# The last third of a hybrid mixer in one written order, and the final norm in two halves of the tokens

## The chip, the cores and the metric

The kernel runs on one NeuronCore of a Trainium2 chip. The metric is the device time of one execution in microseconds (us), the median of three runs. Its engines each work through a queue of their own: TensorE (PE, matrix products), VectorE (DVE), ScalarE (ACT, activations and copies), GpSimd (POOL) and SyncE (SP, which here only issues DMAs). They meet in semaphores: an instruction waits at the head of its queue until what it reads is written and what it overwrites has been read.

## The reference

One decoder layer for 256 tokens of width 1024, all in float32: two half-step SwiGLU feed-forward networks (FFN, 22 tiles of 128 hidden columns) with a mixer between them, each behind an RMSNorm whose scale, shift and gate come from a product of the condition `c` with `w_ada` ("ada", 9 x 1024 columns), and a final RMSNorm.

```
mod = (c @ w_ada + b_ada)                    # 9 x 1024: shift, scale, gate three times
h = modulate(rmsnorm(x, ffn1_norm), sh1, sc1)
x = x + 0.5 * (1 + g1) * swiglu(h, ffn1_w_gate, ffn1_w_up, ffn1_w_down)
h = modulate(rmsnorm(x, mix_norm), sh2, sc2)
x = x + (1 + g2) * hybrid_mixer(h, ...)
h = modulate(rmsnorm(x, ffn2_norm), sh3, sc3)
x = x + 0.5 * (1 + g3) * swiglu(h, ffn2_w_gate, ffn2_w_up, ffn2_w_down)
return rmsnorm(x, final_norm)
```

The mixer projects `h` to attention queries, keys and values, to the input of an mLSTM (a gated linear recurrence, here over chunks of 64 tokens in matrix form) and to a gate `z`. Half of its output is the RMS-normed attention, the other half `(norm(h_m) + mlstm_skip * x_conv) * silu(z)`; both together go through `w_out` (1024 x 1024).

## The kernel before

Everything stands in transposed form: 128 channels on the partitions, 256 tokens on the free axis; `x_sb` is 8 such tiles. A product in float32 is made of three in a faster format (float32r): a weight piece of 128 x 1024 is split into `whi` (ACT, a rounding copy) and `wlo` (DVE, the rest), the activations into `hh` and `hl`, and `mm3` issues hi x hi, lo x hi, hi x lo. `weights()` hands out the next weight chunk (2048 columns, 1 MB), has the DMA of the chunk three ahead issued and splits up to the end of the next chunk; four raw chunks and five pieces each of `whi` and `wlo` have room, so a split waits until the products of five pieces before are done. PSUM has 8 banks under three tags: "b" 2, "m" 2, "a" 4.

The ada products are jobs in a list. `side(0)` takes one out: a DMA of 512 KB (`ada`, three buffers) and one DVE operation that multiplies it with `c` and sums (`junk`, 128 x 1024). FFN 1 works off some, the mixer the rest.

Where `Ordered.on` of an engine is set, its instructions keep the order in which the program issues them (`keep_in_program_order`); where it is off, a scheduler orders them by its own estimate of their times. Either way, each engine then runs its queue in that order. All compute instructions are issued by `call` of `Ordered`, so the trace gives them all line 55, and tiles tell them apart by name.

The last third of the mixer, in program order: `tiles()` projects the z gate, two tiles of 24 matmuls per chunk, with `shifted` as what follows each (a column `col`, `ht` on DVE, `zs` on ACT); `values(1)` is the last projection of attention values (`va`); `turn(3)` transposes attention probabilities (`pT`), `weigh(2)` and `weigh(3)` multiply them with `va` (`oa`) and square; `m_sums` and `m_vars` are the mLSTM's sums for a head (`cn`, `sq`); `a_out` sums the squares over `ones_h` into a bank, takes Ln and Exp (`rl`, `rr`), refines by one Newton step on DVE (`nw`, `rr`), scales `oa` and splits it into `mix0` and `mix3`; `m_factors` makes four rows of factors (`dd`, `vv`, `rs`, `rows`), `z_silu` takes the SiLU of `zs` (another table of ACT), and `m_spread` and `m_out` spread the rows over the partitions and make the mLSTM's half of the output (`cn`, then `hh`, `hl`). The output projection runs over 4 chunks `c` of `w_out`, 48 matmuls each, into 4 banks; then `residual` adds each tile to x and makes `hh`, `hl` and the square for FFN 2, which follows.

In the kernel before, the written order is on from `weigh(3)` to the z tile behind `a_out`, in `m_factors` and from there to `z_silu`, and around `m_spread` and `m_out`; elsewhere in this part the scheduler decides.

At the end, `residual` multiplies x with the final norm's weight on POOL (`u_out`), `rstd_of` makes the norm's factor for all 256 tokens, and five DVE products each send their tiles out, from SP and ACT in turn (L600 to L604).

Of the kernel before, what the change touches and what calls it, by code (L numbers as in the profile page):

```python
# [14 lines left out]
ALU = mybir.AluOpType  # L15
# [46 lines left out]
def layer(ctx: ExitStack, tc: tile.TileContext, i, out: bass.AP):  # L62
# [237 lines left out]
    def rstd_of(parts, ones=None, tag="m", pre=True, mid=None):  # L300

        ps = bank(tag)[:, 0:T]
        for n, s in enumerate(parts):
            pe.matmul(ps, ones_m if ones is None else ones, s, start=(n == 0), stop=(n == len(parts) - 1))
        r = t256("rr", bufs=2)
        l = t256("rl", bufs=1)
        if pre:
            tables("natural_log_exp_and_others")
        act.activation(l, ps, AF.Ln, bias=eps_t)
        act.activation(r, l, AF.Exp, scale=-0.5)  # L310
        if mid:
            mid()
        newton(r, ps, [P, T], "x")
        return r
# [43 lines left out]
            eng.tensor_tensor(acc, acc, s, ALU.add)  # L358
        return s

    def residual(d, ps, g, k):
        dve.scalar_tensor_tensor(x_sb[:, d], ps, g[:, d:d + 1], x_sb[:, d], ALU.mult, ALU.add)
        if k is None:
            s = add_sq(d, pool)
            pool.tensor_scalar(fin_u[0][:, d], x_sb[:, d], sm[:, C_NF + d:C_NF + d + 1], None, ALU.mult)
            return s
        if k == 1:

            s = add_sq(d, pool)
            for j in range(2 * d - 6, 2 * d - 4) if 3 <= d < 6 else range(d, d + 1) if d >= 6 else ():  # L370
                pre_h(k, j)
        elif d == ND - 1:
            s = add_sq(d, pool)
            pre_h(k, d)
        else:
            pre_h(k, d)
            s = add_sq(d, pool)
        return s
# [26 lines left out]
    def ffn(k, nxt):  # L405
        nfa = 3
        with tc.tile_pool(name=f"g{k}", bufs=1) as gp:
            g2 = gp.tile([P, NF, 2, T], F32R, name=f"g2{k}")
            gh, gl = g2[:, :, 0], g2[:, :, 1]
            if k == 0:  # L410
# [71 lines left out]
                        inner(w, f2, ps[2 * j + f2], 0, False)  # L482
                for d in range(4, 8):
                    w = weights()
                    side(1)
                    outer(w, ps, d, d == 7)

                late = [lambda ft=ft: finish(gh, gl, 8 + ft, ps[ft][:, 0:T], ps[ft][:, T:2 * T])
# [1 line left out]
                for j in range(4):  # L490
                    if j < 2:
                        late.pop(0)()
                        late.pop(0)()
                    w = weights()
                    if j == 3:
                        side(1)
                    for f2 in range(2):
                        ft = 2 * j + f2
                        pb = bank("a")
                        inner(w, f2, pb, 4, True)  # L500
                        o = half[:, ft]
                        dve.tensor_tensor(o, o, pb, ALU.add)
                        finish(gh, gl, ft, o[:, 0:T], o[:, T:2 * T])
# [63 lines left out]
    def side(*on):  # L567

        for o in on:
            if jobs:  # L570
                jobs.pop(0)(o)
# [24 lines left out]
    with tc.tile_pool(name="fin", bufs=1) as fp:  # L596
        u = fin_u[0] = fp.tile([P, ND, T], F32, name="u_out")
        jobs += gate_jobs(2)
        ffn(2, None)
        r = rstd_of([acc, nxt_sq[0]], pre=False)  # L600
        r2 = r.unsqueeze(1).to_broadcast([P, 2, T])
        for n, (a, b) in enumerate(((0, 2), (2, 4), (4, 6), (6, 7), (7, 8))):
            dve.tensor_tensor(u[:, a:b], u[:, a:b], r2[:, 0:b - a], ALU.mult)
            (sp, nc.scalar)[n % 2].dma_start(out[:, a:b], u[:, a:b])  # L604


def mixer(tc, nc, i, mp, L):
# [9 lines left out]
    def mt(shape, name, dt=F32, tag=None, bufs=1):  # L617
        return mp.tile(shape, dt, name=nm(name), tag=tag or name, bufs=bufs)

    def tiles(*done):  # L620

        w = weights()
        for g in range(2):
            pb = bank("b")
            for d in range(8):
                mm3(pb[:, 0:W], w, (g * 8 + d) * P, hh[:, d], hl[:, d], start=(d == 0), stop=(d == 7))
            done[g](pb)
            yield

    def shifted(dst):  # L630

        def done(pb):
            col = tmp.tile([P, 1], F32, tag="col", name=nm("col"), bufs=3)
            act.activation(col, pb[:, T:T + 1], AF.Copy)
            t = t256("ht", bufs=3)
            dve.tensor_tensor(t, r, pb[:, 0:T], ALU.mult)
            act.activation(dst, t, AF.Identity, bias=col)
        return done
# [168 lines left out]
    def m_vars(h):  # L807
        pe.matmul(st["prow"][0:4, T:2 * T], ohc[:, h], st["sq", h], start=False, stop=(h == NH - 1),
                  skip_group_check=True)

    def m_factors():


        prow, em = st["prow"], st["em"]
        act.on = dve.on = True
        dd = mt([NH, T], "dd", tag="R2")
        act.activation(dd, prow[0:4, 0:T], AF.Square, scale=EPS ** 0.5)
        dve.tensor_tensor(dd, dd, em, ALU.max)
        vv = mt([NH, T], "vv", tag="R3")
        dve.scalar_tensor_tensor(vv, prow[0:4, T:2 * T], 1.0 / P, dd, ALU.mult, ALU.add)  # L820
        rs = mt([NH, T], "rs", tag="R1")
        act.activation(rs, vv, AF.Ln)
        act.activation(rs, rs, AF.Exp, scale=-0.5)
        newton(rs, vv, [NH, T], "r", 0.0)
        spread(rs)
# [105 lines left out]
            pool.tensor_tensor(acc2, acc2, s, ALU.add)  # L931

    def a_out():
        r2 = rstd_of([acc2, st["osq"]], ones_h, "a", pre=False)
        for j in range(4):
            o = oa[:, j, 0:T]
            dve.scalar_tensor_tensor(o, o, sm[:, C_AN + j:C_AN + j + 1], r2, ALU.mult, ALU.mult)

        mix3[:] = [mt([P, 3, T], name, F32R, tag="pr", bufs=2) for name in ("mix3h", "mix3l")]
        hilo(*mix0, oa[:, 0, 0:T])  # L940
        hilo(*mix3, oa[:, 1:4, 0:T])
# [49 lines left out]
    turn(2)  # L991
    m_scores(3)
    m_sums(1)
    g = tiles(shifted(zs[:, 0]), shifted(zs[:, 1]))
    side(0, 0, 0, 0, 0, 0)
    next(g)
    next(g0)
    turn(3)
    weigh(2)
    for e in (pe, act, dve):  # L1000
        e.on = True
    weigh(3)
    m_sums(2)
    m_vars(0)
    a_out()
    next(g)
    act.on = dve.on = False
    m_sums(3)
    m_skip()
    m_vars(1)  # L1010
# [6 lines left out]
    next(g)  # L1017
    z_silu(0)
    z_silu(1)
    act.on = dve.on = False  # L1020
    po = [bank(t) for t in ("m", "m", "a", "a")]
    for c in range(4):
        w = weights()
        side(*[0] * (0, 1, 2, 3)[c])
        pe.on = c < 2
        for k2 in range(2):
            k = c * 2 + k2
            for d in range(8):
                mm3(po[d // 2][:, (d % 2) * T:(d % 2 + 1) * T], w, (k2 * 8 + d) * P, *mix(k),
                    start=(c == 0 and k2 == 0 and d % 2 == 0), stop=(c == 3 and k2 == 1))  # L1030
                if (k, d) == (1, 7):
                    m_spread()
                    act.on = dve.on = True
                    m_out(0)
                    m_out(1)
                    act.on = dve.on = False
    side(*[0] * len(jobs))
    act.on = dve.on = True
    L["pre_shift"](2)
    act.on = dve.on = False  # L1040
    for d in range(8):
        nxt_sq[0] = residual(d, po[d // 2][:, (d % 2) * T:(d % 2 + 1) * T], L["gt"][1], 2)


# [84 lines left out]
```

## Time and profile before

| | |
|---|---|
| runs | 534.71, 532.76, 532.58 us; median 532.76 |
| profiled execution | 531.47 us |
| its span in the trace | 529.7 us, 9595 instructions |
| mean granted PE clock | 0.995 of full |
| PE, DVE, ACT, POOL busy | 97%, 80%, 53%, 9% |
| FFN 1 begins / mixer's last third / FFN 2 begins / final norm | 0 / about 262 / 329 / 519.3 us |

Times in the trace's rows are in us from the span's start. The busy time of an engine counts the instructions that run, not the queue's waiting. A row of a timeline gives start, duration, engine, operation and tiles (out<-in); in brackets stands how long the engine stood idle ahead of it and which instruction ended that. Matmuls overlap: two in a row start 0.12 us apart and last 0.28 us each.

### The profile page before, as it was taken

How to read it: one execution, taken by the hardware profiler on the slowest of the kernel's cores; microseconds unless marked ns; L12 is line 12 of the kernel's file. 1: busy time of each engine (PE TensorE's matmuls, PEld its weight loads, DVE VectorE, ACT ScalarE, POOL GpSimd, SP SyncE). 2: the span in 40 equal slices, each digit the busy share in tenths (PEclk: the TensorE clock that was granted, in tenths of full speed). 3: DMA queues.
4: the chain of work that ended last, by engine and by line, in shares of the span. 5: the costliest groups of instructions: out<-in, count | busy, mean ns of one | idle time of the engine just before them, and what ended most of it. 6: DMA issues, size and time to landing. Idle time of an engine off the chain costs nothing.

```text
span 529.7 us, 9595 instructions
## 1 busy us (share of the span) xinstructions
PE 511.9 (97%) x3826; PEld 480.0 (91%) x3826; DVE 422.3 (80%) x703; ACT 282.9 (53%) x484; POOL 45.5 (9%) x60
## 2 busy tenths in 40 slices
PE   8999999999999999999999988999999999999992
PEld 7889999999988889988877888999999999988891
DVE  7799977998889997997869887989887777655423
ACT  4364436655645444569766554865555545544410
POOL 5000000000001110120000001300000000022220
PEclk9999999999999999999999999999999999999997
DMA  8999985677878887783115963578764554464002
GB/s 306 363 368 379 376 357 201 251 278 287 321 294 298 335 329 290 282 354 120 41 41 198 400 227 103 206 301 307 285 241 160 171 215 171 161 220 178 0 1 79
DMA packets 24095, 125.73 MB, mean 237 GB/s; under 512 B 2673, under 2 KB 3185, under 8 KB 14578
## 3 DMA queue, kind: packets, MB, share of 16 engines
q1 hardware_dynamic: 23762, 124.72, 62.4%
q8 instruction: 30, 0.49, 0.4%
q10 hardware_dynamic: 288, 0.39, 0.2%
q14 instruction: 15, 0.12, 0.1%
HBM read 124.05 MB, written 1.05 MB: 236 GB/s over the span
## 4 chain that ended last, share of the span: by engine, by line
PE 87%; DVE 6%; DMA 3%; ACT 2%; issue 1%; SPq 0%; DVEq 0%; ACTq 0%
PE psa L55 44%; PE psb L55 24%; PE psm L55 19%; DVE junk L55 2%; DMA ada<-in_ada 2%; DVE wlo L55 1%; ACT whi L55 1%; DMA x<-in_x 1%; DVE u_out L55 0%; DVE ht L55 0%; ACT sq L55 0%; DVE oa L55 0%; DVE hl L55 0%; DVE nw L55 0%; ACT hh L55 0%
## 5 line engine op out<-in xcount | busy, mean ns | idle before, releaser
L55 ACT ACTIVATE whi<-raw 128x1024 fp32r<-128x1024 f32 (+1 forms) x160 | 166.8, 1047 | 128.1 <-PE psa L55 78.7
L55 DVE TENSOR_TENSOR wlo<-raw,whi 128x1024 fp32r<-128x1024 f32 (+1 forms) x160 | 193.7, 1214 | 45.0 <-ACT whi L55 43.5
L55 PE MATMUL psa<-hh,wlo 128*128 128x256 f32 (+1 forms) x440 | 123.3, 281 | 0.0
L55 PE MATMUL psa<-hh,whi 128*128 128x256 f32 (+1 forms) x440 | 123.1, 282 | 0.0
L55 PE MATMUL psa<-hl,whi 128*128 128x256 f32 (+1 forms) x440 | 122.1, 280 | 0.0
L55 DVE SCALAR_TENSOR_TENSOR junk<-ada,c_bc 128x1024 bf16<-128x1024 f32 x72 | 89.8, 1248 | 11.8 <-DMA ada<-in_ada 11.5
L55 PEld LDWEIGHTS psa<-hh,wlo 128*128 128x128 f32 x440 | 83.1, 189 | 0.1
L55 PEld LDWEIGHTS psa<-hh,whi 128*128 128x128 f32 x440 | 82.9, 189 | 0.0
L55 PE MATMUL psb<-hh,whi 128*128 128x258 f32 (+1 forms) x284 | 82.1, 290 | 0.8 <-ACT whi L55 0.6
L55 PEld LDWEIGHTS psa<-hl,whi 128*128 128x128 f32 x440 | 82.7, 189 | 0.0
L55 PE MATMUL psb<-hh,wlo 128*128 128x258 f32 (+1 forms) x284 | 80.5, 284 | 0.4 <-DVE wlo L55 0.4
L55 PE MATMUL psb<-hl,whi 128*128 128x258 f32 (+1 forms) x284 | 79.6, 282 | 0.0
L55 PE MATMUL psa<-g,whi 128*128 128x512 f32 (+1 forms) x198 | 59.8, 369 | 0.0
L55 PEld LDWEIGHTS psb<-hh,whi 128*128 128x128 f32 x284 | 53.7, 189 | 3.0 <-ACT whi L55 1.0
L55 PEld LDWEIGHTS psb<-hh,wlo 128*128 128x128 f32 x284 | 53.8, 189 | 1.7 <-issue 1.0
L55 PEld LDWEIGHTS psb<-hl,whi 128*128 128x128 f32 x284 | 53.5, 190 | 0.0
L55 PE MATMUL psa<-g,wlo 128*128 128x256 f32 x176 | 45.9, 281 | 0.0
L55 PE MATMUL psm<-hh,whi 128*128 128x256 f32 (+1 forms) x156 | 43.9, 282 | 1.7 <-ACT hh L55 1.7
L55 PE MATMUL psm<-hl,whi 128*128 128x256 f32 (+1 forms) x156 | 43.7, 282 | 0.5 <-DVE hl L55 0.4
L55 PE MATMUL psm<-hh,wlo 128*128 128x256 f32 (+1 forms) x156 | 43.8, 281 | 0.0
L55 PEld LDWEIGHTS psa<-g,whi 128*128 128x128 f32 x198 | 35.2, 188 | 6.2
L55 PEld LDWEIGHTS psa<-g,wlo 128*128 128x128 f32 x176 | 32.1, 188 | 0.6
(251 smaller groups left out, 777.5 us busy)
## 6 DMA issues: line engine op xcount, KB each, us to landing
ada<-in_ada SPq DMA_DIRECT2D x72, 512.0 KB, 5.9
raw<-in_dn SPq DMA_DIRECT2D x22, 1024.0 KB, 4.8
raw<-in_guB SPq DMA_DIRECT2D x19, 1024.0 KB, 4.8
raw<-in_gu SPq DMA_DIRECT2D x18, 1024.0 KB, 7.3
raw<-in_gu SPq DMA_DIRECT2D x8, 512.0 KB, 7.4
raw<-in_wqk SPq DMA_DIRECT2D x4, 1024.0 KB, 6.3
raw<-in_wout SPq DMA_DIRECT2D x4, 1024.0 KB, 7.7
raw<-in_guA SPq DMA_DIRECT2D x4, 768.0 KB, 4.6
```

The source lines that it names most:

```text
L55: r = f(*a, **k)
```

## The change

FFN 1 takes three ada products more (one at d = 7, and two in the loop behind it), so that the mixer has three fewer. In the mixer, the written order is on for PE, ACT and DVE from the first z tiles to the end of the residuals, save for ACT while the weights of c = 1 are handed out; `tiles(apart=True)` can be continued between a tile's matmuls and what follows them; the six ada products in a row become single ones at six places, and those of the output projection one per chunk; `m_out(1)` moves to c = 1; the residual takes x of tile d and then the norm's part of tile d - 1 in turn. The final norm is made for 128 tokens at a time, with four products and four DMAs of 256 KB.

```diff
@@ -358,8 +358,9 @@
             eng.tensor_tensor(acc, acc, s, ALU.add)
         return s
 
-    def residual(d, ps, g, k):
-        dve.scalar_tensor_tensor(x_sb[:, d], ps, g[:, d:d + 1], x_sb[:, d], ALU.mult, ALU.add)
+    def residual(d, ps, g, k, add=True):
+        if add:
+            dve.scalar_tensor_tensor(x_sb[:, d], ps, g[:, d:d + 1], x_sb[:, d], ALU.mult, ALU.add)
         if k is None:
             s = add_sq(d, pool)
             pool.tensor_scalar(fin_u[0][:, d], x_sb[:, d], sm[:, C_NF + d:C_NF + d + 1], None, ALU.mult)
@@ -482,7 +483,7 @@
                         inner(w, f2, ps[2 * j + f2], 0, False)
                 for d in range(4, 8):
                     w = weights()
-                    side(1)
+                    side(*[1] * (1 + d // 7))
                     outer(w, ps, d, d == 7)
 
                 late = [lambda ft=ft: finish(gh, gl, 8 + ft, ps[ft][:, 0:T], ps[ft][:, T:2 * T])
@@ -492,7 +493,7 @@
                         late.pop(0)()
                         late.pop(0)()
                     w = weights()
-                    if j == 3:
+                    if j != 1:
                         side(1)
                     for f2 in range(2):
                         ft = 2 * j + f2
@@ -597,11 +598,27 @@
         u = fin_u[0] = fp.tile([P, ND, T], F32, name="u_out")
         jobs += gate_jobs(2)
         ffn(2, None)
-        r = rstd_of([acc, nxt_sq[0]], pre=False)
-        r2 = r.unsqueeze(1).to_broadcast([P, 2, T])
-        for n, (a, b) in enumerate(((0, 2), (2, 4), (4, 6), (6, 7), (7, 8))):
-            dve.tensor_tensor(u[:, a:b], u[:, a:b], r2[:, 0:b - a], ALU.mult)
-            (sp, nc.scalar)[n % 2].dma_start(out[:, a:b], u[:, a:b])
+
+        pr, sq = [bank("m") for _ in range(2)], nxt_sq[0]
+        lr = [t256(t, bufs=b) for t, b in (("rl", 1), ("rr", 2), ("ht", 3))]
+        H = [slice(0, P), slice(P, T)]
+        for e in (pe, act, dve):
+            e.on = True
+        for p, s in zip(pr, H):
+            pe.matmul(p[:, 0:P], ones_m, acc[:, s], start=True, stop=False)
+            pe.matmul(p[:, 0:P], ones_m, sq[:, s], start=False, stop=True)
+        for p, s in zip(pr, H):
+            act.activation(lr[0][:, s], p[:, 0:P], AF.Ln, bias=eps_t)
+            act.activation(lr[1][:, s], lr[0][:, s], AF.Exp, scale=-0.5)
+        for n, (p, s) in enumerate(zip(pr, H)):
+            r, q = lr[1][:, s], lr[2][:, s]
+            dve.scalar_tensor_tensor(q, r, -0.5, r, ALU.mult, ALU.mult)
+            dve.scalar_tensor_tensor(q, p[:, 0:P], EPS, q, ALU.add, ALU.mult)
+            dve.scalar_tensor_tensor(r, q, 1.5, r, ALU.add, ALU.mult)
+            for a, b in ((0, 4), (4, 8)):
+                o = u[:, a:b, s]
+                dve.tensor_tensor(o, o, r.unsqueeze(1).to_broadcast([P, b - a, P]), ALU.mult)
+                (sp, nc.scalar)[a // 4].dma_start(out[:, a:b, s], o)
 
 
 def mixer(tc, nc, i, mp, L):
@@ -617,13 +634,15 @@
     def mt(shape, name, dt=F32, tag=None, bufs=1):
         return mp.tile(shape, dt, name=nm(name), tag=tag or name, bufs=bufs)
 
-    def tiles(*done):
+    def tiles(*done, apart=False):
 
         w = weights()
         for g in range(2):
             pb = bank("b")
             for d in range(8):
                 mm3(pb[:, 0:W], w, (g * 8 + d) * P, hh[:, d], hl[:, d], start=(d == 0), stop=(d == 7))
+            if apart:
+                yield
             done[g](pb)
             yield
 
@@ -812,7 +831,6 @@
 
 
         prow, em = st["prow"], st["em"]
-        act.on = dve.on = True
         dd = mt([NH, T], "dd", tag="R2")
         act.activation(dd, prow[0:4, 0:T], AF.Square, scale=EPS ** 0.5)
         dve.tensor_tensor(dd, dd, em, ALU.max)
@@ -931,7 +949,7 @@
             pool.tensor_tensor(acc2, acc2, s, ALU.add)
 
     def a_out():
-        r2 = rstd_of([acc2, st["osq"]], ones_h, "a", pre=False)
+        r2 = rstd_of([acc2, st["osq"]], ones_h, "a", pre=False, mid=lambda: side(0))
         for j in range(4):
             o = oa[:, j, 0:T]
             dve.scalar_tensor_tensor(o, o, sm[:, C_AN + j:C_AN + j + 1], r2, ALU.mult, ALU.mult)
@@ -991,20 +1009,23 @@
     turn(2)
     m_scores(3)
     m_sums(1)
-    g = tiles(shifted(zs[:, 0]), shifted(zs[:, 1]))
-    side(0, 0, 0, 0, 0, 0)
+    for e in (pe, act, dve):
+        e.on = True
+    g = tiles(shifted(zs[:, 0]), shifted(zs[:, 1]), apart=True)
+    side(0)
     next(g)
     next(g0)
+    next(g)
     turn(3)
     weigh(2)
-    for e in (pe, act, dve):
-        e.on = True
+    side(0)
     weigh(3)
     m_sums(2)
+    side(0)
     m_vars(0)
     a_out()
     next(g)
-    act.on = dve.on = False
+    next(g)
     m_sums(3)
     m_skip()
     m_vars(1)
@@ -1017,12 +1038,14 @@
     next(g)
     z_silu(0)
     z_silu(1)
-    act.on = dve.on = False
     po = [bank(t) for t in ("m", "m", "a", "a")]
     for c in range(4):
+        act.on = c != 1
         w = weights()
-        side(*[0] * (0, 1, 2, 3)[c])
-        pe.on = c < 2
+        act.on = True
+        if c == 1:
+            m_out(1)
+        side(0)
         for k2 in range(2):
             k = c * 2 + k2
             for d in range(8):
@@ -1030,16 +1053,17 @@
                     start=(c == 0 and k2 == 0 and d % 2 == 0), stop=(c == 3 and k2 == 1))
                 if (k, d) == (1, 7):
                     m_spread()
-                    act.on = dve.on = True
                     m_out(0)
-                    m_out(1)
-                    act.on = dve.on = False
     side(*[0] * len(jobs))
-    act.on = dve.on = True
     L["pre_shift"](2)
-    act.on = dve.on = False
-    for d in range(8):
-        nxt_sq[0] = residual(d, po[d // 2][:, (d % 2) * T:(d % 2 + 1) * T], L["gt"][1], 2)
+    x_sb, gt = L["x_sb"], L["gt"]
+    for d in range(9):
+        if d < 8:
+            dve.scalar_tensor_tensor(x_sb[:, d], po[d // 2][:, (d % 2) * T:(d % 2 + 1) * T], gt[1][:, d:d + 1],
+                                     x_sb[:, d], ALU.mult, ALU.add)
+        if d:
+            nxt_sq[0] = residual(d - 1, None, None, 2, False)
+    act.on = dve.on = pe.on = False
 
 
 # ---- launch ----
```

How ACT's queue stands from the last tile of z on. `whi` is the first half of a weight piece's split, `zs` a z tile, `rows` the mLSTM's factors. Of before, from the second last `zs` (the two pieces of c = 1, `whi_3646` and `whi_3650`, stand 7 and 2 rows further up; `whi_3720` and `whi_3724` are of c = 2, `whi_3782` is the first of c = 3):

```order
L55 ACTIVATE zs_2553<-ht_3590,col_3588 128x256
L55 ACTIVATE dd_3594<-psa_3310 4x256
L55 ACTIVATE whi_3720<-raw_3553 128x1024
L55 ACTIVATE rs_3599<-vv_3597 4x256
L55 ACTIVATE rs_3599<-rs_3599 4x256
L55 ACTIVATE whi_3724<-raw_3553 128x1024
L55 ACTIVATE rows_2541<-rs_3599 4x256
L55 ACTIVATE col_3633<-psb_3608 128x1
L55 ACTIVATE whi_3782<-raw_3644 128x1024
L55 ACTIVATE zs_2553<-ht_3635,col_3633 128x256
L55 ACT_TABLE_LOAD
L55 ACTIVATE zs_2553<-zs_2553 128x512 x2
```

Of after, the same stretch (`whi_3650` and `whi_3654` are of c = 1, the next two of c = 2):

```order
L55 ACTIVATE rows_2554<-rs_3603 4x256
L55 ACTIVATE col_3637<-psb_3612 128x1
L55 ACTIVATE zs_2566<-ht_3639,col_3637 128x256
L55 ACT_TABLE_LOAD
L55 ACTIVATE zs_2566<-zs_2566 128x512 x2
L55 ACTIVATE whi_3650<-raw_3392 128x1024
L55 ACTIVATE whi_3654<-raw_3392 128x1024
L55 ACTIVATE whi_3723<-raw_3557 128x1024
L55 ACTIVATE whi_3727<-raw_3557 128x1024
L55 ACTIVATE hh<-cn_2563 128x2x256 x2
```

The pieces that stood between the operations on `rs` and ahead of the table load stand behind both `silu`, and those of c = 1 are now the first of them.

ACT's queue at the start of FFN 2, where x gets its residual. `whi_4023` is a piece of FFN 2 and `whi_3981` the last but one. Of before:

```order
L55 ACTIVATE hh<-cn_2550 128x2x256
L55 ACTIVATE hh<-sh_155 128x8 x2
L55 ACTIVATE whi_3981<-raw_3780 128x512
L55 ACTIVATE hh<-x,gs_152 128x256
L55 ACTIVATE sq_3916<-x 128x256
L55 ACTIVATE hh<-x,gs_152 128x256
L55 ACTIVATE sq_3922<-x 128x256
L55 ACTIVATE hh<-x,gs_152 128x256
L55 ACTIVATE sq_3928<-x 128x256
L55 ACTIVATE whi_4023<-raw_3846 128x1024
L55 ACTIVATE hh<-x,gs_152 128x256
```

Of after:

```order
L55 ACTIVATE whi_3977<-raw_3788 128x1024
L55 ACTIVATE hh<-sh_155 128x8 x2
L55 ACTIVATE whi_3981<-raw_3788 128x512
L55 ACTIVATE whi_4023<-raw_3851 128x1024
L55 ACTIVATE hh<-x,gs_152 128x256
L55 ACTIVATE sq_3917<-x 128x256
L55 ACTIVATE hh<-x,gs_152 128x256
L55 ACTIVATE sq_3923<-x 128x256
L55 ACTIVATE hh<-x,gs_152 128x256
```

The piece `whi_4023` stood behind three pairs of `hh` and `sq`; now it stands ahead of the first.

DVE's queue around the norm of the attention (`nw`, `rr`, `oa`) and the split into `mix0l` and `mix3l`. Of before:

```order
L55 SCALAR_TENSOR_TENSOR junk_3390,mod<-ada_3388,c_bc 128x1024
L55 SCALAR_TENSOR_TENSOR junk_3394,mod<-ada_3392,c_bc 128x1024
L55 SCALAR_TENSOR_TENSOR nw_3491<-rr_3487 128x256
L55 SCALAR_TENSOR_TENSOR junk_3398,mod<-ada_3396,c_bc 128x1024
L55 SCALAR_TENSOR_TENSOR nw_3491<-psa_3484,nw_3491 128x256
L55 SCALAR_TENSOR_TENSOR rr_3487<-nw_3491,rr_3487 128x256
L55 SCALAR_TENSOR_TENSOR oa_2555<-oa_2555,sm,rr_3487 128x256 x4
L55 TENSOR_TENSOR wlo_3647<-raw_3400,whi_3646 128x1024
L55 TENSOR_TENSOR mix0l_2552<-oa_2555,mix0h_2551 128x256
L55 TENSOR_TENSOR mix3l_3500<-oa_2555,mix3h_3499 128x768
L55 TENSOR_TENSOR ht_3532<-rr_2424,psb_3505 128x256
```

Of after:

```order
L55 SCALAR_TENSOR_TENSOR junk_3461,mod<-ada_3459,c_bc 128x1024
L55 SCALAR_TENSOR_TENSOR junk_3481,mod<-ada_3479,c_bc 128x1024
L55 SCALAR_TENSOR_TENSOR junk_3493,mod<-ada_3491,c_bc 128x1024
L55 SCALAR_TENSOR_TENSOR nw_3495<-rr_3487 128x256
L55 SCALAR_TENSOR_TENSOR nw_3495<-psa_3484,nw_3495 128x256
L55 SCALAR_TENSOR_TENSOR rr_3487<-nw_3495,rr_3487 128x256
L55 SCALAR_TENSOR_TENSOR oa_2568<-oa_2568,sm,rr_3487 128x256 x4
L55 TENSOR_TENSOR mix0l_2565<-oa_2568,mix0h_2564 128x256
L55 TENSOR_TENSOR mix3l_3504<-oa_2568,mix3h_3503 128x768
L55 TENSOR_TENSOR ht_3536<-rr_2437,psb_3509 128x256
```

The ada product between the Newton steps stands ahead of them, and the weight piece behind `oa` (`wlo_3647`) is gone from here.

## Rows read from the trace of the kernel before

**Rows 1.** The page, part 1: busy us (share of the span) and instructions.
```profile
PE 511.9 (97%) x3826; PEld 480.0 (91%) x3826; DVE 422.3 (80%) x703; ACT 282.9 (53%) x484; POOL 45.5 (9%) x60
```

**Rows 2.** Windows: stretch, length, busy (instructions) of PE, PEld, DVE, ACT, POOL; PEclk, DMA, GB/s.
```profile
280.00:300.00 20.00, 19.22 (x141) 15.85 (x140) 18.79 (x34) 11.53 (x27) 1.14 (x1) 1.00 0.83 312
300.00:320.00 20.00, 18.39 (x149) 17.72 (x148) 16.79 (x26) 10.95 (x17) 0.00 (x0) 1.00 0.65 240
320.00:340.00 20.00, 18.21 (x147) 17.69 (x146) 16.89 (x31) 14.41 (x29) 6.16 (x7) 1.00 0.33 113
```

**Rows 3.** PE's timeline, 262 to 330 us: start, duration, engine, line, operation, tiles.
```profile
266.17 0.37 PE L55 MATMUL psb<-hl,whi 128*128 128x258 f32 x1
266.38 0.28 PE L55 MATMUL psb<-hh,whi 128*128 128x258 f32 x1
266.50 0.28 PE L55 MATMUL psb<-hh,wlo 128*128 128x258 f32 x1
...
284.62 1.63 PE L55 MATMUL psa<-pT,va 128*64 128x256 f32 x16 [0.60 <-ACT va L55]
...
288.73 0.59 PE L55 MATMUL psa<-sq,ones_h 128*128 128x256 f32 x2
...
294.40 0.39 PE L55 MATMUL psb<-hh,whi 128*128 128x258 f32 x1
...
308.36 0.92 PE L55 MATMUL psb<-rows,ohr 36*128 36x256 f32 x4 [1.24 <-DVE rows L55]
...
323.15 0.39 PE L55 MATMUL psm<-hh,whi 128*128 128x256 f32 x1 [1.67 <-ACT hh L55]
...
329.26 0.28 PE L55 MATMUL psb<-hh,whi 128*128 128x258 f32 x1
```

**Rows 4.** DVE's timeline, 286 to 330 us.
```profile
291.79 1.22 DVE L55 SCALAR_TENSOR_TENSOR junk<-ada,c_bc 128x1024 bf16<-128x1024 f32 x1 [1.04 <-DMA ada<-in_ada]
...
305.40 1.23 DVE L55 TENSOR_TENSOR wlo<-raw,whi 128x1024 fp32r<-128x1024 f32 x1 [0.43 <-ACT whi L55]
...
307.79 0.41 DVE L55 TENSOR_TENSOR rows<-rs,rows 4x256 fp32r<-4x256 f32 x1
...
310.43 0.69 DVE L55 TENSOR_TENSOR cn<-cn,xc 128x512 f32<-128x512 f32 x1
```

**Rows 5.** ACT's timeline, 286 to 330 us.
```profile
289.87 0.42 ACT L55 ACTIVATE rr<-rl 128x256 f32<-128x256 f32 x1
...
307.15 1.06 ACT L55 ACTIVATE whi<-raw 128x1024 fp32r<-128x1024 f32 x1 [1.44 <-PE psa L55]
...
309.23 1.28 ACT L55 ACT_TABLE_LOAD   x1
310.52 1.16 ACT L55 ACTIVATE zs<-zs 128x512 f32<-128x512 f32 x2
...
327.94 0.51 ACT L55 ACTIVATE hh<-x,gs 128x256 fp32r<-128x256 f32 x1 [0.59 <-DVE x L55]
```

**Rows 6.** Lines by form for `xc` on ACT: count, ns min/median/max, first and last start.
```profile
L55 ACT ACTIVATE xc<-xc,sm x4: 510/521/554, 266.5 to 278.9; 128x256 f32<-128x256 f32 x4
```

**Rows 7.** Waits, 80 to 150 us: us in total, times, longest.
```profile
ACT whi L55 <- PE psa L55: 18.2, 17, 1.8
```

**Rows 8.** Timeline of the end, 519 to 530 us.
```profile
519.75 0.70 PE L55 MATMUL psm<-sq,ones_m 128*128 128x256 f32 x2 [0.65 <-ACT sq L55]
...
522.88 2.56 DVE L55 TENSOR_TENSOR u_out<-u_out,rr 128x512 f32<-128x512 f32 x5
...
524.21 1.27 ACTq L604 DMA_DIRECT2D out<-u_out  x2
```

**Rows 9.** DMA issues: queue, count, KB each, median us from issue to landing.
```profile
out<-u_out SPq DMA_DIRECT2D x2, 256.0 KB, 2.9
```

**Rows 10.** Windows at the end, columns as in Rows 2.
```profile
523.00:524.00 1.00, 0.00 (x0) 0.00 (x0) 1.00 (x2) 0.00 (x0) 0.00 (x0) 1.00 0.00 0
524.00:525.00 1.00, 0.00 (x0) 0.00 (x0) 1.00 (x3) 0.00 (x0) 0.00 (x0) 0.52 0.50 184
```

## The prediction

> **What bounds the kernel now.** I read the page's busy shares first: TensorE (PE) is busy in 97% of the span [rows 1], so a change can win only where PE stands still, at the two ends, or in the little that PE loses between matmuls of different kinds. Then the stretches of 20 us around the part that is rewritten: PE is busy for 19.22, 18.39 and 18.21 us of them [rows 2]; 0.78 + 1.61 + 1.79 = 4.18 us of standing still is all that this stretch holds. Then PE's timeline, which names the waits: 0.60 us for `va` at 284.62, 1.24 us for `rows` at 308.36, 1.67 us for `hh` at 323.15 [rows 3], the rest in smaller pieces. FFN 2 begins at 329.26, behind the last product of the output projection, without a wait. So the question is whether the written order removes these 4.2 us or puts other waits there. Last, the end of the kernel: from PE's last work (519.75 + 0.70) on, nothing hides anything [rows 8].
>
> The times below are those of the profiled execution (531.47 us, span 529.7); the median of the runs shown is 532.76, 1.29 us more, and I add that at the end.
>
> **Three products moved into FFN 1.** Each is a DMA of 512 KB and a `junk` of 1.22 us on VectorE (DVE) [rows 4], 3.7 us in all. There ACT waits for PE before splitting the next weight piece, 17 times and 18.2 us in 70 us [rows 7]: the pieces are ready ahead of PE, and that lead hides the 3.7 us. I cost it at nothing; if the lead gave out, up to 3.7 us would show. The mixer loses the same 3.7 us of DVE, counted in the walk below.
>
> **Up to the sum of the attention squares (S, the second matmul against `ones_h`).** The same 1,982 matmuls stand before S in both orders. Before, the 24-matmul blocks of the projections are cut by other work: from the first block of `values(1)` to S there are 18 runs of one kind or the other, now 10. A cut costs the gap between 266.17 and 266.38 (0.21 us) instead of that to the next (0.12) [rows 3], so 0.1 to 0.2 us with both its edges: 8 fewer are 0.8 to 1.6 us. The wait for `va` (0.60), where ACT had a weight piece ahead of it, should go too, though `weigh(3)` now waits some 0.5 us for `pT` behind other work in ACT's fixed order. Bounds: 0.6 to 2.7 us; I take 1.8, and S moves from 288.73 to 286.9.
>
> **From S to the output projection.** ACT's `rr` ends 1.56 us behind S (289.87 + 0.42 - 288.73) [rows 3, 5]: 288.5 now. Before, a product that waited 1.04 us for its DMA stood in the middle of the Newton steps [rows 4] and a weight piece behind `oa`; now the products stand ahead. Three Newton steps, four scalings and the splits into `mix` with the first `ht` take 5.3 us: `ht` of the second z tile is done at 293.8. This is a new wait: by the allocation the third z tile now takes the bank that this `ht` frees. PE would reach it at S + 5.67 (294.40 - 288.73 before [rows 3]) = 292.6, and waits 1.2 us. With the 24-matmul blocks unchanged, PE then ends the first chunk of the output projection and `m_spread` at 307.2, where the next chunk (c = 1) began at 309.2 before (308.36 + 0.85): 2.0 us ahead so far, the 1.24 us for `rows` included, since `rows` is done at 305.1 (below).
>
> **The next chunk's weights (c = 1).** Here I expect the gain to be lost. ACT's queue, now in written order, from 293.8: `zs` 0.5, `cn` and `sq` 0.7, the four `xc` scalings 2.1 (4 x 0.52 [rows 6]; before, they ran between 266.5 and 279), two weight pieces 1.9, to 299.0; DVE's two `wlo` and the `ht` behind them (1.15 + 1.15 + 0.35) to 300.7; `zs`, then the chain `dd`, `vv`, `rs` twice, three Newton steps, `rows`, nine operations of about 0.45 (0.41 [rows 4] and the step between engines), to 305.1; `ht` and `zs` to 306.0; the table load 1.29 to 307.3; two `silu` 1.15 to 308.45 [rows 5]. Only behind that stand the two pieces of this chunk's weights; before, they were made ahead of all this, and so were both pieces of chunk 2 and the first of chunk 3, that one at 307.15 [rows 5]. `whi` 0.97 to 309.4, `wlo` 1.2 to 310.6: PE's second matmul of this chunk waits from 307.3 to 310.6, 3.4 us (one matmul comes in between). With that PE is 1.3 us behind the kernel before (309.2 + 0.12 there).
> On a point of this chain the Trainium skill says otherwise (ScalarE: Activation LUTs, "What ACT_TABLE_LOAD costs"): it gives 1.28 us for the load and 1.38 us more for a drain. The trace has the load at 309.23 and the next activation at 310.52 [rows 5], so no drain beside it. By the page the wait at c = 1 would be 1.4 us longer and the time 536.6, inside the range of my own case below; the trace speaks against it, and I keep its 1.29 and give the page's figure no more than a tenth of that case.
>
> **Chunks 2 and 3.** PE ends c = 1 at 316.4. DVE behind 310.6: the second `wlo` and a `junk` (1.15 each), three `cn` at 0.72 a step, `hh` on ACT 0.6, `hl` 0.6, then `wlo` 1.2 of c = 2 [rows 4]: 317.6, a wait of 1.2 us. PE ends c = 2 at 323.3; DVE has a `wlo`, three `cn`, `hl`, a `junk` and, after `hh` and `whi` on ACT, the `wlo` of c = 3, at 324.5: 1.1 us more. These replace the 0.37 us for `hl` and the 1.67 us for `hh` of before. c = 3 ends at 330.2.
>
> **FFN 2's first matmul.** In ACT's written order a weight piece of FFN 2 stands ahead of the first `hh` of x, and its buffer is free only when the last matmul of c = 3 has read it. So: 330.35 (end of that matmul), `whi` 0.97, `hh` 0.51 [rows 5], about 332.0. Before, the first `hh` was made at 327.94 and the piece later, and FFN 2 began at 329.26 [rows 3]: +2.7 us. The first `hl` (behind that piece's `wlo`, 332.8) is wanted by the ninth matmul, 0.96 us later: hidden, or 0.3 us. I know of no later wait: PE is the slower in FFN 2 from here.
>
> **The final norm.** In two halves, Ln and Exp of 128 columns lie between the 0.17 us of a one-column operation and the 0.42 us of 256 columns, I take 0.3; the first half's `rr` is there at 520.95 instead of 521.41. On DVE three Newton steps of 0.33 and two products of 0.65 per half (2.56 us for the same elements before [rows 8]) end at 523.25 and 525.55; before it was 525.44. Two DMAs are out at 522.6 and 523.2; the last is 256 KB, 2.9 us to landing [rows 9], where the last two were 128 KB and also left at about 525.4 [rows 8]. Change -0.4; bounds -1.0 (both halves overlap better) and +0.5 (the same bytes go out in runs of 512 bytes, which no row here shows).
>
> **Sum.** FFN 1 0, mixer +2.7, end -0.4: +2.3 to +2.5, or 533.9 by the profile and **535.2 us** beside the median. An S at 286.0 or 288.0 shifts all of it by -0.9 or +1.1, and everything behind `rr` hangs on S. Own range of this case 533 to 537.5. A measurement of this kernel can tell about 0.5% (2.7 us) from no change, and this sum (+0.45%) lies at that bound.
>
> **Rivals.**
> (a) The order does what it says: the products are out of the way, the weights of c = 1 come in time, all 4.18 us of waits go, with the saved cuts (1.4) and 0.4 at the end: 532.76 - 6.0 = 526.8. For it: the attention's norm is done 5 us earlier, and DVE has 3.7 us less to do. Against it: ACT's queue as counted above would have to be 3.4 us shorter at `silu`, and the first `hh` of FFN 2 has to overtake.
> (b) Half of that: the chain behind `rr` runs 2 us shorter than I count (S at 286.0, small operations at 0.40), the wait at c = 1 falls to about 1.5 us, and with the bubble at FFN 2 nothing is won or lost: 532.8.
> (c) On the other side: the wait at c = 1, 3.4 us with one matmul in it, lowers PE's clock. The trace shows the granted clock at 1.00 in 523:524, 3 us after PE's last work, and 0.52 in 524:525 [rows 10], that is 1.2 GHz instead of 2.4. It decides if the granted clock of any stretch behind 307 reads under 1.00. At the lower level a matmul takes 0.24 us instead of 0.12; how soon the level comes back is not shown here, so the price lies between 0 and one chunk (48 x 0.12 = 5.8 us). I take half: +2.9, or 538.
> The Trainium skill (TensorE: Matmul & The Clock Gate, "Part 1: The HAM clock gate") has the same two levels and an idle array put back to the lower one; the tail's rows agree. By it (c) is possible, though the lone matmul and the short wait speak against it.
>
> **How the numbers follow.** My case 0.52, of which 0.28 above the 2.7 us bound and 0.24 inside; (a) 0.25, all faster; (b) 0.11, no change; (c) 0.12, slower. So faster 0.25, same 0.35, slower 0.40. The range of 8 in 10 goes from 527 (half of (a) is left out) to 539 (a late S, or (c) with more than half a chunk); the likeliest's own range stands above.
>
> **What would show it.** Right: PE waiting about 3 us for `whi` and `wlo` at the second chunk of the output projection, some 1 us for `ht` at the third z tile, 1.7 us for `hh` at the start of FFN 2, and none for `va` and `rows`; S near 286.9; DVE's last product ending about 2.8 us later than the 525.4 of before, the start of the final norm having moved by 2.7. Wrong: idle in the three stretches no longer than 4 us; S later than 288; waits for `wlo` in FFN 1 (the lead gone); granted clock under 1.00 near 310.

## The result, and the profile after

The changed kernel takes 535.91 us (median of 11 runs, 535.51 to 537.93) against 533.71 us before in the same comparison: ratio 1.0051, 95% interval 1.0032 to 1.0070. One of the 11 runs of before, at 2846.87 us, is not in the ratio. The changed kernel is slower by about half a per cent, close to the 535.2 us that were forecast. The profiled execution of after has a span of 534.1 us, 4.4 us more than that of before, which was one of the faster runs of its kernel (531.47 us, where most of its runs lie between 531 and 537).

Windows of after, columns as in [rows 2]; the last four lines are four pieces of the second:

```profile
280.00:300.00 20.00, 18.25 (x129) 14.45 (x128) 13.28 (x22) 12.46 (x28) 0.83 (x1) 1.00 0.48 185
300.00:320.00 20.00, 16.50 (x125) 15.96 (x124) 12.79 (x20) 9.63 (x17) 0.00 (x0) 0.91 0.36 132
320.00:340.00 20.00, 17.46 (x143) 16.85 (x141) 19.05 (x34) 12.56 (x25) 4.85 (x6) 1.00 0.50 185
...
312.00:313.00 1.00, 0.44 (x2) 0.45 (x3) 1.00 (x2) 1.00 (x2) 0.00 (x0) 0.51 0.00 0
313.00:314.00 1.00, 1.00 (x6) 1.00 (x6) 1.00 (x2) 1.00 (x2) 0.00 (x0) 0.50 0.07 16
314.00:315.00 1.00, 1.00 (x6) 1.00 (x6) 1.00 (x3) 0.09 (x1) 0.00 (x0) 0.50 0.31 92
315.00:316.00 1.00, 1.00 (x9) 1.00 (x8) 0.96 (x2) 0.00 (x0) 0.00 (x0) 0.79 0.83 301
```

PE stands still for 1.75 + 3.50 + 2.54 = 7.8 us in the three stretches, where it was 4.2 [rows 2], and the granted clock is at its lower level for some 3 us. PE's timeline of after says where (the rows with a wait, and those that answer to [rows 3]):

```profile
284.90 1.25 PE L55 MATMUL psa<-pT,va 128*64 128x256 f32 x8 [0.56 <-ACT pT L55]
...
288.64 0.59 PE L55 MATMUL psa<-sq,ones_h 128*128 128x256 f32 x2
...
295.54 0.39 PE L55 MATMUL psb<-hh,whi 128*128 128x258 f32 x1 [1.16 <-DVE ht L55]
...
307.94 0.73 PE L55 MATMUL psb<-rows,ohr 36*128 36x256 f32 x4
...
311.30 0.38 PE L55 MATMUL psm<-mix3h,whi 128*128 128x256 f32 x1 [2.62 <-ACT whi L55]
312.56 0.58 PE L55 MATMUL psm<-mix3h,wlo 128*128 128x256 f32 x1 [0.88 <-DVE wlo L55]
312.94 0.41 PE L55 MATMUL psm<-mix3l,whi 128*128 128x256 f32 x1
313.15 0.41 PE L55 MATMUL psm<-mix3h,whi 128*128 128x256 f32 x1
...
326.27 0.39 PE L55 MATMUL psm<-hh,wlo 128*128 128x256 f32 x1 [0.78 <-DVE wlo L55]
...
333.69 0.39 PE L55 MATMUL psb<-hh,whi 128*128 128x258 f32 x1 [1.59 <-ACT hh L55]
```

The waits for `va` and `rows` are gone, and those at c = 1 (2.62 and 0.88 us) and at the start of FFN 2 (1.59 us) are new. Behind the wait at c = 1, thirteen steps from one matmul to the next (312.56 to 315.47) take 2.91 us, most of them 0.21 us; at 0.12 us each they would take 1.56. Place by place, against [rows 3]: S is 0.09 us earlier; S to the third z tile takes 1.23 us more (the wait for `ht`); from there to `m_spread` 1.56 us less; from `m_spread` to the second matmul of c = 1 3.55 us more (4.62 instead of 1.07, by the row of before below); and from there to FFN 2 1.30 us more. That is +4.43 us at the start of FFN 2 (333.69 for 329.26). In PE's timeline of before:

```profile
309.43 0.27 PE L55 MATMUL psm<-mix3h,wlo 128*128 128x256 f32 x1
```

ACT's timeline of after at c = 1 and at the start of FFN 2 shows both causes:

```profile
307.33 0.51 ACT L55 ACTIVATE zs<-ht,col 128x256 f32<-128x256 f32 x1 [0.89 <-DVE ht L55]
307.86 1.28 ACT L55 ACT_TABLE_LOAD   x1
309.15 1.15 ACT L55 ACTIVATE zs<-zs 128x512 f32<-128x512 f32 x2
310.20 3.88 ACT L55 ACTIVATE whi<-raw 128x1024 fp32r<-128x1024 f32 x4
...
332.19 1.06 ACT L55 ACTIVATE whi<-raw 128x1024 fp32r<-128x1024 f32 x1 [2.18 <-PE psa L55]
333.15 0.49 ACT L55 ACTIVATE hh<-x,gs 128x256 fp32r<-128x256 f32 x1
```

The piece of c = 1 starts when the last `silu` is done, and the first `hh` of x when the piece ahead of it is done, which itself waited for PE's last matmul of c = 3. In [rows 5] the load stood at 309.23 with the pieces of c = 1 and 2 and the first of c = 3 already made, and `hh` at 327.94.

The end of the kernel, from the start of the last x to the span's end, takes 10.5 us in after (from 523.63) and 11.0 before, where the last x stands in DVE's timeline at 518.70:

```profile
518.70 0.48 DVE L55 SCALAR_TENSOR_TENSOR x<-psa,gt,x 128x256 f32<-128x256 f32 x1 [6.81 <-PE psa L55]
```

In after:

```profile
525.23 0.39 PE L55 MATMUL psm<-sq,ones_m 128*128 128x128 f32 x2
525.60 0.31 ACT L55 ACTIVATE rr<-rl 128x128 f32<-128x128 f32 x1
...
528.20 0.28 DVE L55 SCALAR_TENSOR_TENSOR ht<-rr 128x128 f32<-128x128 f32 x1
...
529.17 1.29 DVE L55 TENSOR_TENSOR u_out<-u_out,rr 128x512 f32<-128x512 f32 x2
```

DVE's last product ends at 530.46, 6.83 us behind the start of the last x; before it was 6.74 [rows 8]. What is won is won behind it, on the last DMA's way: 3.6 us to the span's end instead of 4.2.

### The profile page after: what moved, and what is told of

Its sections match the earlier page's. It is cut to its first block, busy times and chain, and to the rows that moved or that the text cites. A ratio compares the mean times of both kernels' runs of the same rounds, so it can differ in the third digit from the quotient of the medians.

```text
span 534.1 us, 9606 instructions
## 1 busy us (share of the span) xinstructions
PE 512.9 (96%) x3830; PEld 481.6 (90%) x3830; DVE 421.6 (79%) x705; ACT 283.6 (53%) x486; POOL 47.0 (9%) x60
## 4 chain that ended last, share of the span: by engine, by line
PE 84%; DVE 8%; ACT 4%; DMA 2%; issue 1%; DVEq 0%; ACTq 0%
PE psa L55 43%; PE psb L55 24%; PE psm L55 18%; DVE wlo L55 2%; DVE junk L55 2%; DMA ada<-in_ada 2%; ACT whi L55 1%; DVE ht L55 1%; DVE cn L55 1%; ACT zs L55 1%; ACT hh L55 0%; DVE c_hl L55 0%; DVE u_out L55 0%; DVE hl L55 0%; ACT xc L55 0%
```

## The experiments

Eleven runs, in four groups, each beside runs of the kernel before on the same chip. The changed kernel was not run again beside them. Where a run's median is set against its 535.91 us, the runs were on different chips; the kernel before had medians of 533.6 to 533.9 us in these comparisons, and 532.71 in the one of the last run, `mixed4`.

**The parts alone: the final norm.** `tail_only` is the kernel before with the last hunk of the diff; `no_tail` is the changed kernel without it.

> The kernel before with the final norm in two halves alone. My theory: the end of the kernel, from the last x to the span's end, is 11.0 us before and 10.5 us in the changed kernel, so 0.5 us less: ratio 0.999. Rival (runs of 512 bytes cost more, or the halves only add instructions): 0 to 0.5 us more, and the end takes 11 us or longer.

> The changed kernel with the final norm as before. My theory: FFN 2 begins as in the changed kernel (333.7), and the end takes 11.0 instead of 10.5 us: 0.5 us above the changed kernel, ratio to the kernel before 1.006. Rival (the halves cost): below the changed kernel.

Measured: `tail_only` 1.0015 (0.9987 to 1.0042), `no_tail` 1.0082 (1.0053 to 1.0110), which is 1.1 us over the changed kernel by the medians. Most of the 1.1 us is not the norm: the runs of both kernels fall into two groups, three and three of `no_tail` (536.0 to 536.3 and 537.9 to 538.4), seven and four of the changed kernel (535.5 to 536.0 and 537.3 to 537.9), and group beside group the difference is 0.3 to 0.5 us. The end takes 10.51 us in the first run and 10.98 in the second. So the halves win about 0.5 us by the traces; by the times of `tail_only` alone that can't be told, since its runs vary by 5 us (531.7 to 536.4), as do those of before beside it. Its one trace, of a run of 535.54 us, shows a reason. DVE's and PE's timelines of `tail_only` (ahead of the edit's place, where its code is that of before), and then PE's of before at the same matmul:

```profile
293.35 1.23 DVE L55 SCALAR_TENSOR_TENSOR junk<-ada,c_bc 128x1024 bf16<-128x1024 f32 x1 [2.45 <-DMA ada<-in_ada]
```

```profile
299.81 0.39 PE L55 MATMUL psb<-hh,whi 128*128 128x258 f32 x1 [1.74 <-DVE ht L55]
```

```profile
298.25 0.39 PE L55 MATMUL psb<-hh,whi 128*128 128x258 f32 x1 [0.18 <-DVE ht L55]
```

The product between the Newton steps waited 2.45 us for its DMA, where it was 1.04 in [rows 4], PE waited 1.74 us for `ht` instead of 0.2, and the granted clock fell behind that (0.55 in 300:302, 0.59 in 302:304), and once more behind the 1.67 us for `hh` (0.88, 0.50 and 0.77 in 326:332), where it stayed at 1.00 in the profile of before. The kernel before has a weak place here that its one profile hardly showed.

**The parts alone: three products in FFN 1.**

```diff
-                    side(1)
+                    side(*[1] * (1 + d // 7))
...
-                    if j == 3:
+                    if j != 1:
```

> The kernel before with the three ada products moved to FFN 1 alone. My theory: no wait of PE in 40 to 160 us, and the mixer, relieved of 3.7 us of DVE, about the same or up to 1 us shorter: FFN 2 begins between 328.3 and 329.3. Rival (DVE in FFN 1 is short of time): waits of PE for wlo in 80 to 160 us, up to 2 us, and FFN 2 that much later.

Measured: 0.9957 (0.9935 to 0.9979), faster by 2.3 us. PE is busy for 20.00 us of 20 in each stretch from 40 to 140 us: FFN 1 does hide the 3.7 us of DVE. FFN 2 begins at 327.31, 1 us below what I expected: with fewer products among the `cn` steps on DVE, PE's 1.67 us for `hh` at c = 3 are gone.

**What the fall of the clock costs.** The changed kernel, with this in PE's queue behind `m_spread`:

```diff
+                    fill = bank("a")
+                    for _ in range(20):
+                        pe.matmul(fill[:, 0:P], ones_h, ones_h, start=True, stop=True)
```

> The changed kernel with 20 matmuls of 128 columns, whose result nobody reads, in PE's queue where it waits for the weights of c = 1. In the changed kernel the granted clock reads 0.51, 0.50, 0.50 and 0.79 in 312 to 316, behind that wait, and 14 matmuls start 0.21 instead of 0.12 us apart, 1.3 us in all. Theory A: the fall of the clock lengthens the path: the granted clock stays at 1.00, FFN 2 begins 1.3 us earlier (332.4). Theory B: DVE's chain (it works without a gap from 311.3 on) sets the end of this part: the clock stays at 1.00, but PE's wait for wlo at c = 3 grows from 0.8 to about 2.1 us and FFN 2 begins at 333.7 as before. I hold B the likelier, 0.65 to 0.35.

Measured: 1.0049 (1.0024 to 1.0074), median 535.64. The clock stays up, in windows of `fill`:

```profile
312.00:314.00 2.00, 2.00 (x20) 2.00 (x19) 2.00 (x3) 1.88 (x2) 0.00 (x0) 1.00 0.00 0
314.00:316.00 2.00, 2.00 (x19) 2.00 (x18) 1.93 (x5) 0.00 (x0) 0.00 (x0) 1.00 0.67 194
```

and PE's timeline of `fill`:

```profile
312.89 0.36 PE L55 MATMUL psm<-mix3h,whi 128*128 128x256 f32 x1
...
319.21 0.39 PE L55 MATMUL psm<-hh,wlo 128*128 128x256 f32 x1 [0.27 <-DVE wlo L55]
...
326.07 0.39 PE L55 MATMUL psm<-hh,wlo 128*128 128x256 f32 x1 [0.91 <-DVE wlo L55]
...
333.40 0.39 PE L55 MATMUL psb<-hh,whi 128*128 128x258 f32 x1 [1.59 <-ACT hh L55]
```

The filling lasted longer than the wait: the second matmul of c = 1 starts at 313.09, and counted from S (288.44 in this run) that is 0.7 us later than in after. So 0.7 of the 1.3 us that the full clock gives went into the filling, and 0.4 us into waits for `wlo` (0.27 + 0.91 instead of 0.78). FFN 2 begins 0.3 us earlier, of which 0.2 stood already at S. So in this run the fall cost next to nothing: B, though the test is less sharp than planned. `res_late` below, which keeps the wait and whose edit comes only behind c = 3, says the same more sharply:

```profile
300.00:320.00 20.00, 16.51 (x112) 15.97 (x111) 12.79 (x20) 9.44 (x16) 0.00 (x0) 0.83 0.38 132
```

The clock's mean in this stretch is 0.83, where after has 0.91, so the lower level lasted about twice as long; yet the last matmul of c = 3 starts only 0.4 us later behind S than in after, and the wait for `wlo` at c = 3 is gone. Whether the fall costs more in other runs is not shown. 4 of the 11 runs of the changed kernel lie at 537.3 to 537.9 with a mean clock of 0.985, the other 7 at 535.5 to 536.0 with 0.989 to 0.992, and with the filling 8 of 9 lie at 535.5 to 535.9. But no trace of one of the four was kept, and 11 of the 12 runs of `res_late` lie at 534.3 to 534.7, with mean clocks of 0.986 to 0.992.

**The weights of c = 1 earlier.** The changed kernel, with

```diff
     m_factors()
+    w0 = weights()
     next(g)
...
-        w = weights()
+        w = weights() if c else w0
```

> The changed kernel, but the split of the weights of c = 1 is issued behind the factors' rows and ahead of the last z tile's ht, zs, table load and silu. My theory: PE's wait at c = 1 (2.6 + 0.9 us) falls below 0.4, the granted clock stays at 1.00 there, and part of it comes back as waits for wlo at c = 2 (about 1.8) and c = 3 (about 1.1), because silu and cn are later; FFN 2 begins at about 330.6 instead of 333.7: 3 us, or ratio 0.998 to 1.000 to the kernel before. Rival (DVE's chain alone sets the pace behind rr): FFN 2 begins at 333 or later, ratio 1.004.

Measured: 0.9994 (0.9971 to 1.0017), 533.0 us, 2.9 us below the changed kernel. PE's timeline of `c1_early`, all its waits from 305 us on but a small one for `hl`:

```profile
310.01 0.50 PE L55 MATMUL psb<-rows,ohr 36*128 36x256 f32 x2 [1.68 <-DVE ht L55]
...
322.66 0.39 PE L55 MATMUL psm<-hh,wlo 128*128 128x256 f32 x1 [0.44 <-DVE wlo L55]
...
329.96 0.39 PE L55 MATMUL psb<-hh,whi 128*128 128x258 f32 x1 [1.59 <-ACT hh L55]
```

The wait at c = 1 is gone, the clock stays at 1.00, and FFN 2 begins 3.7 us earlier. What came back came at another place than expected: the last `ht` now stands behind two `wlo` on DVE, and the second half of `m_spread` needs the bank that this `ht` frees.

**FFN 2's piece behind the third tile of x.** The changed kernel, with

```diff
+    L["split_piece"]()
     L["pre_shift"](2)
...
+        if d == 1:
+            L["split_piece"]()
         if d:
             nxt_sq[0] = residual(d - 1, None, None, 2, False)
+        if d == 3:
+            L["split_piece"]()
```

> The changed kernel, but the weight piece of FFN 2 that stood ahead of the first hh of x is issued behind x's third tile. My theory: PE's wait for hh at the start of FFN 2 (1.6 us) falls to about 0.6, since DVE's x is itself made just when c = 3 ends; FFN 2 begins at 332.7, 1.0 us less, and the piece is there in time; ratio 1.003. Rival (the piece is then late): the 1 us comes back as a wait for whi or wlo in 336 to 342, ratio 1.005.

Measured: 1.0026 (1.0007 to 1.0046), 534.48 us. FFN 2 begins at 332.53, with 0.23 us of waiting for `hh`, and no wait follows in FFN 2: the piece was early enough. That is 1.4 us less of waiting, 1.4 us by the medians, and 1.2 us at the start of FFN 2.

**Both edits, and a third.** `both` has the two edits above; `both_ht` has in addition the second z tile's `ht` directly behind the Newton step:

```diff
     def a_out(g):
         r2 = rstd_of([acc2, st["osq"]], ones_h, "a", pre=False, mid=lambda: side(0))
+        next(g)
+        next(g)
         for j in range(4):
```

> The changed kernel with both edits, the early split for c = 1 and the late piece of FFN 2. My theory: the two add up, FFN 2 begins at about 329.9, as in the kernel before (329.3), and with the end 0.5 us shorter the ratio is 0.996 to 0.999. Rival (what one gives the other takes): no better than the better one of the two alone.

> As with both edits, and the ht of the second z tile goes to DVE directly behind the last Newton step, ahead of the scalings of oa and the split into mix. My theory: PE's wait for ht (1.2 us at 295.5) goes, and the chain behind it is up to 1 us earlier: FFN 2 begins at about 328.9, ratio 0.994 to 0.998. Rival (oa, later by 0.35 us, holds the chain): FFN 2 begins as with both edits.

Measured: `both` 0.9953 (0.9933 to 0.9974), 531.08 us; `both_ht` 0.9943 (0.9923 to 0.9964), 530.29 us. The two edits add up (2.9 and 1.4 us alone, 4.8 together, a little more than expected): both new waits were on the path, and without them the change is faster than the kernel before. The third takes the 1.16 us for the first `ht` away; at `m_spread` the wait for the other `ht` is 2.12 us instead of 1.68, so part comes back, and the profiled run's FFN 2 even began later (329.78 against 329.25), with the clock lowered behind that wait; that run, 531.56 us, is one of the two slowest of its twelve. The medians differ by 0.8 us.

**The weak place of the kernel before.** Its code, with the sixth product behind the scalings of `oa`:

```diff
-    side(0, 0, 0, 0, 0, 0)
+    side(0, 0, 0, 0, 0)
...
     a_out()
+    side(0)
```

> The kernel before, with five ada products where six stood and the sixth behind the scalings of oa. In the run of the kernel before with half-norms alone, the product between the Newton steps waited 2.45 us for its DMA (0.24 us more ahead of it), PE then waited 1.74 us for ht, and the granted clock fell behind it. My theory: this DMA is why the kernel before takes 531 to 537 us from run to run: without it in the Newton steps PE's wait for ht is below 0.5 us, the runs lie within 531 to 533.5, and the median is 1 to 2 us lower, ratio 0.996 to 0.999. Rival (the spread has its cause elsewhere, at the waits for rows and hh): the same spread and ratio 1.000.

Measured: 0.9970 (0.9950 to 0.9990), 532.06 us, runs from 531.0 to 534.9 where those of before beside it lay from 532.2 to 536.6. PE has no wait for `ht` any more; those for `rows` and `hh` are as before. So the place costs time, 1.8 us by the medians, and the rival's ratio of 1.000 is ruled out. The spread hardly shrank (3.9 us from lowest to highest, 4.4 before): how much of it the DMA makes is not shown.

**The best written order.** As `both_ht`, with the first half of c = 1 split between the factors' Newton steps and `rows`, the second behind the last `zs`:

```diff
         newton(rs, vv, [NH, T], "r", 0.0)
+        L["split_piece"]()
         spread(rs)
...
     m_factors()
-    w0 = weights()
     next(g)
+    w0 = weights()
```

> As the changed kernel with all three edits, and the first half of the weights of c = 1 is split between the Newton steps of the factors and rows, the second behind the last z tile's ht and zs. My theory: PE's wait for that ht at m_spread (2.1 us) falls below 0.3, and FFN 2 begins 1 to 2 us earlier, at 326.5 to 328: ratio 0.990 to 0.993. Rival (silu and the weights of c = 2 on DVE hold the next step): the 2 us come back as waits for wlo at c = 2, ratio 0.994 to 0.996.

Measured: 0.9938 (0.9915 to 0.9961), 530.78 us: the rival's case. The wait at `m_spread` is gone (0.11 us are left), and PE waits at c = 2 instead, in its timeline (of a run of 532.16 us, the slowest of the seven):

```profile
313.74 0.38 PE L55 MATMUL psm<-hh,whi 128*128 128x256 f32 x1 [0.30 <-ACT hh L55]
315.60 0.39 PE L55 MATMUL psm<-hh,wlo 128*128 128x256 f32 x1 [1.48 <-DVE wlo L55]
```

The times do not tell it from `both_ht` (0.9943).

**The parts without the written order.** The kernel before with the three products in FFN 1, the final norm in halves, and `side(0, 0, 0, 0)` where six stood, one more behind `a_out()`.

> The kernel before with the scheduler's order in the mixer, but with the three ada products in FFN 1, four products where six stood and one behind the scalings of oa, and the final norm in halves. My theory: the products moved to FFN 1 are worth 2 us without any written order (FFN 2 at 327.3 in that run, although a DMA still waited in the Newton steps there), so without that wait FFN 2 begins at 326 to 327, the end takes 10.5 us, and the ratio is 0.989 to 0.993, as good as the best written order or better. Rival (only a written order gets under 0.994): ratio 0.995 to 0.997.

Measured: 0.9928 (0.9903 to 0.9954), 529.76 us: the lowest ratio of all, though its interval overlaps those of the three best written orders (0.9938 to 0.9953). PE's timeline, all its waits from 285 us to the end of the mixer:

```profile
307.82 0.92 PE L55 MATMUL psb<-rows,ohr 36*128 36x256 f32 x4 [1.24 <-DVE rows L55]
...
317.46 0.38 PE L55 MATMUL psm<-hl,whi 128*128 128x256 f32 x1 [0.36 <-DVE hl L55]
```

FFN 2 began at 327.98 in this run, 1 us later than expected, with the clock at 0.50 to 0.74 in 308 to 312, behind the wait for `rows`. The ratio is within what was expected. So no written order was needed to come as far; that this one is better than the best of them is not shown.

## Why the prediction was right, point by point

- The three products in FFN 1 cost nothing: right, by `ffn1_only`. That they win 2.3 us by themselves in the scheduler's order was not seen, since I only walked the written order. (Four single products stand in the changed code where the six stood, not six as the section on the change says.)
- S at 286.9: wrong, the step of the sum that failed. S came at 288.64, 0.09 us earlier than before instead of 1.8. The terms named there give less than 1.8 by themselves: 1.2 for the cuts (the middle of 0.8 to 1.6) and 0.60 for `va`, less 0.5 for `pT`, are 1.3. And two of the three were mis-sized. The transposes of `turn(3)` ended only 0.6 us earlier (283.44 for 284.02): the eight cuts saved were worth under 0.1 us each, not 0.1 to 0.2. And `pT` cost 1.06 us, not 0.5, counted from the first product with `va` to the first of the next kind, in PE's timelines of after and of before (row 284.62 in [rows 3]):

```profile
283.47 0.88 PE L55 MATMUL psa<-pT,va 128*64 128x256 f32 x8
286.08 0.92 PE L55 MATMUL psm<-wE,vm 128*128 128x256 f32 x4
```

```profile
286.17 0.92 PE L55 MATMUL psm<-wE,vm 128*128 128x256 f32 x4
```

  That is 2.61 us for the sixteen products, where it was 1.55. The 0.56 us that the timeline gives as idle are half of it; the eight products behind the wait are also spread over 1.18 us, while the second of the two copies of `pT` on ACT ends at 285.23.
- From S to the third z tile: right (1.16 us for `ht`, forecast 1.2), and with it the waits for `va` and `rows` that go.
- c = 1: right in place, cause and size (2.62 + 0.88 = 3.5 us, forecast 3.4), and shown by taking the cause away: `c1_early` is 2.9 us faster by the medians. The table load took 1.28 us and the next activation stood at 309.15, 1.29 behind its start: again no drain beside it, against the rule of the Trainium skill (ScalarE: Activation LUTs, "What ACT_TABLE_LOAD costs") that was weighed there.
- Chunks 2 and 3: forecast 1.2 and 1.1 us, measured 0 and 0.78. At the lower clock PE came later to where DVE would have let it wait: most of the time was spent at the slower matmuls instead (1.35 us). At the full clock, in `fill`, the waits were 0.27 and 0.91.
- FFN 2's start: right in place and cause (1.59 us, and 0.17 for `hl`). `res_late` takes 1.4 us of it away.
- The final norm: -0.5 us by the traces, forecast -0.4.
- Rival (c) came true in its condition: the granted clock fell behind the wait at c = 1 (0.51 in 312:313), which the prediction held unlikely. Its price did not: a matmul step took 0.21 us there, not 0.24, the level was back at 1.00 before half the chunk was done, and by `fill` and `res_late` the fall cost little in the runs that were profiled. Rival (a) fell by the waits; it is what the edits reach in part (0.9938 to 0.9953), with the order mended at the places named. Rival (b) wanted S at 286.0.
- Of the prediction's signs of being wrong, two came, the late S and the clock under 1.00 near 310, and DVE's last product ended 5.0 us later than before (530.46 for 525.44), not 2.8. PE's waits, which are the mechanism, came where the prediction has them, save the one at c = 2.
- That the time came within 0.7 us of the forecast is luck in part. The walk gave 533.9 us for the profiled execution, which took 535.91: 2.0 us too little, and the late S (1.7 us) is most of that. I then added 1.29 us, by which the profiled run of before lay under the median of three; the profiled run of after lies at its own median (535.91), so nothing in it answers to this addition, which made up for most of the miss. For the same reason the profiles differ by 4.4 us and the comparison of all runs by 0.51%, about 2.7 us.

## What to carry to other kernels

A written order fixes not only what it was made for: each engine's queue also fixes what stands ahead of the next operand of the bottleneck. Here the weights of c = 1 behind a table load and two SiLUs, and one weight piece ahead of the first tile of the next stage, took more than the removed waits gave; both waits show if one follows the queue of each feeding engine up to the next matmul that reads from it. Time the parts of a change singly: the two lines in FFN 1 were worth 2.3 us, and the rest of the change hid them.

## What the runs showed of the hardware

PE's granted clock (1.00 is its level of 2.4 GHz, 0.50 that of 1.2) fell after shorter rests than I had thought from the tail, where it stayed up until about 3.5 us after PE's last work [rows 8, 10]. In `tail_only` it read 0.55 in the 2 us behind a wait of 1.74 us, in `both_ht` 0.73 and then 0.50 behind one of 2.12 us, in `mixed4` 0.74 and 0.50 behind one of 1.24 us; in the profiled run of before it stayed at 1.00 behind waits of 1.24 and 1.67 us. `c1_early` and `both` have the same order up to the end of c = 3 and the same wait of 1.68 us at 310 us; windows of the first, then of the second:

```profile
300.00:320.00 20.00, 18.32 (x151) 17.86 (x150) 15.43 (x24) 10.46 (x19) 0.00 (x0) 1.00 0.47 164
```

```profile
300.00:320.00 20.00, 18.32 (x138) 17.85 (x137) 15.43 (x24) 10.46 (x19) 0.00 (x0) 0.91 0.46 163
```

So the same wait lowers the clock in one run and not in another. How much of the 1 to 2 us by which runs of one kernel differ comes from that is not shown: in `mixed4` three runs with a mean clock of 0.993 to 0.996 lie 1.1 to 1.5 us below the five with 0.990 and 0.991, while in `both` the runs with 0.990 and those with 0.995 or 0.996 all lie at 530.7 to 531.1.
